# A two-layer mixer trunk: masks built first, v copied out raw before one gelu over four token tiles, and the last pair's combination moved behind a tile of u

## The chip, the cores and the metric

The kernel runs on one core of one Trainium2 chip. The metric is device time in microseconds for one execution. Besides the times there is one execution that was taken with the hardware profiler; its instruction times are what the rest of this text reads.

## The reference, cut to what matters

The program is a trunk of two residual layers over 1024 tokens of width 1024, all in float32. Layer 0 mixes the tokens in two ways that share one input projection: a gated MLP over chunks of 128 tokens (`u`, `v`), and a sliding-window attention with 8 heads and three branches of window and dilation (128, 1), (512, 4) and (2048, 16), whose outputs are weighted by the softmax of their log-denominators. The change touches only this layer's mixer.

```python
h = rms_norm(x, norm_mix_g)
# token mixer A: chunked gMLP spatial gating
u, v = gelu(u), gelu(v)
vn = layer_norm(v, ln_g, ln_b).reshape(Bn, nc, A_CHUNK, A_GROUPS, A_GROUP_DIM)
ws = where(tril, w_s, 0)
mixed = einsum('gts,bnsgc->bntgc', ws, vn) + b_s.T[:, :, None]
a = u * mixed.reshape(Bn, S, A_WIDTH)
# token mixer B: one output and one log-denominator per branch
outs, lses = dilated_branch(q, k, v, window, dilation) for each branch
b = einsum('rbhs,rbhsc->bhsc', softmax(stack(lses), axis=0), stack(outs))
x = x + concat(a, b) @ w_out
```

Behind the mixer each layer has a gated MLP with a causal convolution; layer 1 has a gated linear attention in place of this mixer.

## The kernel before, in words

Tokens are tiled by 128 (eight tiles, `NT`), the width by 128 too. Every float32 matmul operand is split into a high and a low part of a faster type (`split`, L98–101: the high part is a cast on ScalarE, L100, the low part a subtraction on VectorE, L101; for weights with a gain L105 and L106), and a product is made of three matmuls (`mm_tok`, L182–190). A scheduler orders the instructions of each engine at compile time; where `keep_in_program_order` is called on an instruction, it stays where the program has it among its engine's instructions.

`even` (L509–538) is the mixer of layer 0. It loads x, transposes it into `hq`, and then `attention` (L597–797) runs four pairs of heads. At its head stand the masks (L606–628): a memset, two GpSimd selects, an iota and nine more VectorE instructions make `mband` (window of 128) and `mboth` (the second and third branch together in the order of stride 4, where a key that both hold is counted twice). For each pair `project` (L673–732) makes q, k and v of a token tile (tile `pj`), normalises and transposes them (`tq`, `tk`), and runs the near-window attention of that tile through `unit` and `scores` (L634–667): scores in `sc`, mask and row minimum on VectorE (L643), the exponential on ScalarE (L644), transposes (`pP`, L658), and the product with v (`po`, L666). `dilated` (L734–749) does the same over the dilated order and stores its result to DRAM (`od`), from where it is read back in token order (`on`, L781). `combine` (L751–772) puts the near and the dilated part together for a group of four token tiles: the smaller of the two parts' row minima (`cM`, L756, kept in program order), differences (`cE`, L759), one exponential (L760), weights (`cD`, L763–766), two multiplications, one on GpSimd and one on VectorE (L769), an addition (L771) and a store to `bcat` in DRAM (L772). A pair's combination runs inside the next pair's projection; the last pair's is called behind the loop.

Then `gmlp` (L550–586) projects v tile by tile: gelu from PSUM on ScalarE (L567), layer normalisation (L569–576, with a power on GpSimd, L140/L141), and for each half of four tiles eight gating matmuls (`pm`, L581) whose bias adds write the result back into `mx` (L582). `u_proj` (L588–595) projects u (`pu`), takes its gelu (L592, `ut`) and multiplies it into `mx` (L593). The scheduler lets these projections overlap with the last pair's attention.

The output projection `out_first` (L434–458) reads `cat` back from `bcat` (L1110), transposes `mx` and `cat` (`pc`, L442), splits them into `hq` and multiplies with `wo` (`po`, L190 through L425). SyncE's queue (SP) issues all of these loads and stores in one order. Pools in PSUM: `pt` two buffers, `sc` two, `pj` two, `po` one, `tq` one; `pm` shares `sc` with the scores, `pc` follows in a later pool.

Of the kernel before, what the change touches and what calls it, by code (L numbers as in the profile page):

```python
# [19 lines left out]
P = 128  # L20
# [22 lines left out]
def f32(ap):  # L43
    return ap.bitcast(F32)
# [11 lines left out]
def trunk(ctx: ExitStack, tc: tile.TileContext, a, out):  # L56
# [452 lines left out]
    def even(gm_open):  # L509
        with ExitStack() as st:  # L510
            pools = {}
            for tag, bufs in (("pt", 2), ("sc", 2), ("pj", 2), ("po", 1), ("tq", 1)):
                pools[tag] = st.enter_context(tc.tile_pool(name="ps_" + tag, bufs=bufs, space=PSUM, reuse_waits="tile"))
            ps = Tagged(pools)
            pq = st.enter_context(tc.tile_pool(name="pq", bufs=1, reuse_waits="tile"))
            par0 = ExitStack()
            pq0 = par0.enter_context(tc.tile_pool(name="pq0", bufs=1, side="right", reuse_waits="tile"))
            with tc.tile_pool(name="nrm", bufs=1, reuse_waits="tile") as pool:
                for n in range(NT):
                    xt = pool.tile([P, D], F32, tag="x", bufs=3, name=f"x0{n}")  # L520
                    Q.dma_start(xt, rows(a["x"], n))
                    if n == 0:
                        Q.dma_start(g0, a["norm_mix_gT"])
                    for g in range(2):
                        pt = ps.tile([P, 4, P], F32, tag="pt", name=f"pt{n}{g}")
                        for j in range(4):
                            k = 2 * j + g
                            T.transpose(pt[:, j, :], xt[:, k * P : (k + 1) * P], ident)
                        split(place(hq[g][n // 4], n), pt)
                    if n == 1:  # L530
                        wq0 = load_qkv(0)
                    h = pool.tile([P, D], F32, tag="h", bufs=2, name=f"h{n}")
                    ssq = small.tile([P, 1], F32, tag="ssq", name=f"ssq{n}")
                    A.activation(h, xt, AF.Square, accum_out=ssq)
                    inv_rms(ssq, 1, D, f"rn{n}", r0[:, n : n + 1])
            with tc.tile_pool(name="at", bufs=2, reuse_waits="tile") as at, \
                    tc.tile_pool(name="av", bufs=1, reuse_waits="tile") as av:
                return attention(ps, at, av, pq, pq0, par0, wq0, gm_open)

    def load_qkv(p):  # L540
        return [w for kp in range(4)
# [8 lines left out]
    def gmlp(ps, gm):  # L550

        wv = load_half(a["w_vu"][0], "wv", g0)
        lnG = gm.tile([P, 512], F32, name="lnG")
        Q.dma_start(lnG, a["ln_g"].partition_broadcast(P))
        lnB = gm.tile([P, 512], F32, name="lnB")
        Q.dma_start(lnB, a["ln_b"].partition_broadcast(P))
        bs = gm.tile([P, GROUPS], F32, name="bs")
        Q.dma_start(bs, a["a_bs"])
        ws = gm.tile([P, GROUPS, P], F32, name="ws")
        Q.dma_start(ws, a["a_ws"])  # L560

        G.affine_select(out=ws, in_=ws, compare_op=ALU.is_ge, fill=0.0, base=0,
                        pattern=[[0, GROUPS], [1, P]], channel_multiplier=-1)

        def consume(n, pj):
            gv = gm.tile([P, 512], F32, tag="gv", bufs=2, name=f"gv{n}")
            A.activation(gv, pj, AF.Gelu, scale=r0[:, n : n + 1])  # L567
            st = small.tile([P, 6], F32, tag="bn", name=f"bn{n}")
            V.bn_stats(st, gv)  # L569
            mv = small.tile([P, 2], F32, tag="mv", name=f"mv{n}")  # L570
            V.bn_aggr(mv, st)
            r = inv_rms(mv[:, 1:2], 1, 1, f"lr{n}")
            V.tensor_scalar(gv, gv, mv[:, 0:1], r, op0=ALU.subtract, op1=ALU.mult)
            V.tensor_mul(gv, gv, lnG)
            half, j = n // 4, n % 4
            V.tensor_add(mx[half][:, j, :], gv, lnB)
            if j == 3:
                for g in range(GROUPS):
                    gc = mx[half][:, :, g * 64 : g * 64 + 64]
                    pm = ps.tile([P, 4, 64], F32, tag="sc", name=f"pm{half}{g}")  # L580
                    T.matmul(pm, ws[:, g, :], gc, start=True, stop=True)  # L581
                    V.tensor_scalar(gc, pm, bs[:, g : g + 1], None, op0=ALU.add)  # L582

        mx = [gm.tile([P, 4, 512], F32, name=f"mx{h}") for h in range(2)]
        proj512(ps, wv, "pv", consume)
        return [mx[n // 4][:, n % 4, :] for n in range(NT)]

    def u_proj(ps, gm, mixed):  # L588

        def consume(n, pj):  # L590
            t = gm.tile([P, 512], F32, tag="gv", bufs=2, name=f"ut{n}")
            A.activation(t, pj, AF.Gelu, scale=r0[:, n : n + 1])  # L592
            V.tensor_mul(mixed[n], mixed[n], t)  # L593

        proj512(ps, load_half(a["w_vu"][1], "wu", g0), "pu", consume)

    def attention(ps, at, av, pq, pq0, par0, wq0, gm_open):  # L597

        gqk = pq.tile([P, 2, 2, 64], F32, name="gqk", bufs=1)
        for s in range(2):  # L600
# [1 line left out]
            Q.dma_start(gqk[:, 1, s, :], a["k_g"].partition_broadcast(P))  # L602
        V.tensor_scalar(gqk[:, 0], gqk[:, 0], -0.125, None, op0=ALU.mult)
        gqk = gqk.rearrange("p a s c -> p (a s c)")

        mband = at.tile([P, 2 * P], F32, name="mband", bufs=1)  # L606
        V.memset(mband, 0.0)
        G.affine_select(out=mband[:, :P], in_=mband[:, :P], compare_op=ALU.is_ge, fill=BIG, base=0,
                        pattern=[[1, P]], channel_multiplier=-1)
        G.affine_select(out=mband[:, P:], in_=mband[:, P:], compare_op=ALU.is_ge, fill=BIG, base=0,  # L610
                        pattern=[[-1, P]], channel_multiplier=1)

        di = at.tile([P, 2 * P], I32, tag="sm", name="di", bufs=3)
        G.iota(di, pattern=[[-1, 2 * P]], base=P, channel_multiplier=1)
        V.tensor_scalar(di, di, 3, None, op0=ALU.bitwise_and)
        m16 = at.tile([P, 2 * P], F32, tag="sm", name="m16", bufs=3)
        V.tensor_copy(m16, di)
        V.tensor_scalar(m16, m16, BIG, None, op0=ALU.mult)  # L620
        V.tensor_tensor(m16[:, P:], m16[:, P:], mband[:, P:], op=ALU.max)
        mboth = at.tile([P, 2 * P], F32, name="mboth", bufs=1)
        V.tensor_tensor(mboth, mband, m16, op=ALU.min)
        count = at.tile([P, 2 * P], F32, tag="sm", name="count", bufs=3)
        V.tensor_scalar(count, mband, 1.0, None, op0=ALU.is_lt)
        V.tensor_scalar(m16, m16, 1.0, None, op0=ALU.is_lt)
        V.tensor_mul(count, count, m16)
        V.scalar_tensor_tensor(mboth, count, -math.log(2.0), mboth, op0=ALU.mult, op1=ALU.add)

        def by4(t):  # L630

# [119 lines left out]
        def combine(p, g, os):  # L751

            nm = [o[:, :, 128:130] for o in os]
            den = [o[:, :, 130:132] for o in os]
            M = small.tile([P, 4, 2], F32, tag="cM", bufs=2, name=f"cM{p}{g}")
            tc.keep_in_program_order(V.tensor_tensor(M, nm[0], nm[1], op=ALU.min))  # L756
            e = small.tile([P, 2, 4, 2], F32, tag="cE", bufs=2, name=f"cE{p}{g}")
            for i in range(2):
                V.tensor_sub(e[:, i], M, nm[i])  # L759
            A.activation(e, e, AF.Exp)  # L760
            dd = small.tile([P, 2, 4, 2], F32, tag="cD", bufs=2, name=f"cD{p}{g}")
            for i in range(2):
                V.tensor_mul(dd[:, i], e[:, i], den[i])  # L763
            V.tensor_add(dd[:, 0], dd[:, 0], dd[:, 1])
            V.reciprocal(dd[:, 1], dd[:, 0])
            V.tensor_tensor(e, e, dd[:, 1:2].to_broadcast([P, 2, 4, 2]), op=ALU.mult)
            for i, eng in ((0, G), (1, V)):
                ov = os[i][:, :, :P].rearrange("p n (s c) -> p n s c", s=2)
                eng.tensor_tensor(ov, ov, e[:, i, :, :, None].to_broadcast([P, 4, 2, 64]), op=ALU.mult)  # L769
            o0, o1 = (o[:, :, :P] for o in os)  # L770
            V.tensor_add(o0, o0, o1)  # L771
            Q.dma_start(bcat[g].rearrange("(n p) c -> p n c", p=P)[:, :, p * P : p * P + P], o0)  # L772

        made = project(0, wq0)
        for p in range(PAIRS):
# [3 lines left out]
            for g in range(2):  # L779
                on = at.tile([P, 4, 132], F32, tag="on", name=f"on{p}{g}", bufs=2)  # L780
                Q.dma_start(on, od.rearrange("(n p) c -> p n c", p=P)[:, 4 * g : 4 * g + 4, :])  # L781
                ons.append(on)

            def then(g):
                combine(p, g, [os[g], ons[g]])

            if p + 1 < PAIRS:
                made = project(p + 1, then=then)
            else:
                then(0)  # L790
                then(1)
            if p + 2 == PAIRS:
                par0.close()
                gm = gm_open()
        mixed = gmlp(ps, gm)
        u_proj(ps, gm, mixed)
        return mixed


# [448 lines left out]
```

## Time and profile before

| | before |
|---|---|
| median of 3 runs | 2196.88 us (2196.64 to 2197.8) |
| profiled execution | 2204.97 us |
| its span | 2203.2 us |
| mean granted TensorE clock | 0.992 |

The profile counts from the first to the last instruction of the program (the span). Rows of groups read: line, engine, operation, output and inputs with their shapes, count, then busy microseconds, mean nanoseconds, and the idle time ahead of them with what ended it. A row of the timeline begins with its start and its duration in microseconds. PEld is TensorE's loading of weights, which overlaps its matmuls. The granted clock is the share of the full rate that TensorE was given.

### The profile page before, as it was taken

The page shows a single profiled execution, that of the slowest core. Times are in us where ns is not written, and L with a number is a line of the kernel's source. Part 1 is how long each engine was busy: PE and PEld are TensorE (multiplying, and loading weights), DVE is VectorE, ACT ScalarE, POOL GpSimd, SP SyncE. Part 2 cuts the span into 40 slices and gives each one's busy share as a digit, 9 for nine tenths or more (in the row PEclk, how much of TensorE's full clock was granted, in tenths as well). Part 3 has the DMA queues.
Part 4 walks back from the last instruction along what each step waited for, and adds up shares of the span by engine and source line. Part 5 has one row for each costly group of instructions (what it writes and reads, how often), then busy time and mean ns, then how long its engine had stood idle before and what let it go on. Part 6 is the DMA issues. An engine that isn't in the chain of part 4 may idle for free.

```text
span 2203.2 us, 29873 instructions
## 1 busy us (share of the span) xinstructions
PE 2152.2 (98%) x10508; PEld 1820.2 (83%) x10508; DVE 1532.8 (70%) x2459; ACT 1045.5 (47%) x2006; POOL 488.0 (22%) x519
## 2 busy tenths in 40 slices
PE   7999998999999999999999999999999999999999
PEld 7999987887888888878889787878788888888887
DVE  5566654457888888845577777657787878885554
ACT  6546564345444444434453555534544444454443
POOL 4444420002333342200010011110232424320000
PEclk9999998999999999999999999999999999999999
DMA  4122212565545444575563133377544444457555
GB/s 140 51 73 80 72 42 79 174 237 181 163 158 164 159 148 161 187 281 180 202 232 113 67 99 102 105 250 267 195 139 158 154 165 158 169 176 269 204 197 195
DMA packets 157254, 349.59 MB, mean 159 GB/s; under 512 B 17408, under 2 KB 54272, under 8 KB 156720
## 3 DMA queue, kind: packets, MB, share of 16 engines
q1 hardware_dynamic: 157104, 347.68, 47.1%
q8 instruction: 83, 1.36, 0.3%
q14 instruction: 67, 0.55, 0.1%
HBM read 239.02 MB, written 108.59 MB: 158 GB/s over the span
## 4 chain that ended last, share of the span: by engine, by line
PE 83%; DMA 5%; DVE 5%; ACT 3%; issue 3%; POOL 1%; SPq 0%; ACTq 0%; DVEq 0%; POOLq 0%
PE puB L290 11%; PE pgB L290 11%; PE pgC L290 5%; PE puC L290 5%; PE pv L190 5%; PE pj L190 5%; PE pdC L397 5%; PE pdB L397 5%; PE pdO L397 4%; PE po L190 4%; PE puA L290 3%; PE pgA L290 2%; PE pdP L397 2%; PE pdQ L397 2%; PE pBq L960 2%
## 5 line engine op out<-in xcount | busy, mean ns | idle before, releaser
L101 DVE TENSOR_TENSOR da<-ar,da 128x512 fp32r<-128x512 f32 x154 | 106.3, 691 | 159.7 <-ACT da L100 159.7
L100 ACT CAST da<-ar 128x512 fp32r<-128x512 f32 x154 | 96.1, 624 | 214.3 <-PE pdC L397 98.3
L190 PE MATMUL po<-wo,hq 128*128 128x512 f32 x768 | 183.7, 394 | 1.6 <-ACT hq L100 0.9
L190 PEld LDWEIGHTS po<-wo,hq 128*128 128x128 f32 x768 | 141.7, 188 | 30.7 <-DVE hq L101 1.5
L190 PE MATMUL pj<-wq,hq 128*128 128x384 f32 x768 | 156.3, 349 | 2.2 <-ACT vN L698 1.2
L190 PE MATMUL pv<-wv,hq 128*128 128x512 f32 (+2 forms) x768 | 141.1, 340 | 2.4 <-DVE b L992 1.6
L397 PE MATMUL pdB<-dw,da 128*128 128x512 f32 x528 | 136.4, 391 | 2.1 <-ACT dw L100 2.1
L190 PEld LDWEIGHTS pj<-wq,hq 128*128 128x128 f32 x768 | 134.1, 193 | 3.9 <-ACT vN L698 2.0
L397 PE MATMUL pdC<-dw,da 128*128 128x512 f32 x528 | 136.8, 392 | 0.0
L190 PEld LDWEIGHTS pv<-wv,hq 128*128 128x128 f32 x768 | 118.7, 189 | 17.6 <-DVE b L992 2.1
L397 PEld LDWEIGHTS pdB<-dw,da 128*128 128x128 f32 x528 | 98.7, 188 | 23.4 <-ACT dw L100 2.5
L397 PEld LDWEIGHTS pdC<-dw,da 128*128 128x128 f32 x528 | 99.7, 189 | 20.7
L140 POOL TENSOR_SCALAR rn<-ssq 128x1 f32<-128x1 f32 x24 | 9.3, 386 | 478.9 <-ACT h L148 248.2
L256 POOL TENSOR_TENSOR S1g<-rg 128x512 f32<-128x512 f32 x20 | 29.2, 1462 | 384.0 <-DMA wsd<-D 251.3
L101 DVE TENSOR_TENSOR dw<-wr,dw 128x512 fp32r<-128x512 f32 x154 | 105.9, 688 | 8.6 <-ACT dw L100 8.1
L397 PE MATMUL pdO<-dw,da 128*128 128x512 f32 x396 | 102.4, 390 | 0.0
L100 ACT CAST dw<-wr 128x512 fp32r<-128x512 f32 x154 | 95.1, 617 | 11.5 <-DMA wr<-in_w_dn 7.5
L397 PEld LDWEIGHTS pdO<-dw,da 128*128 128x128 f32 x396 | 74.5, 188 | 15.6
L319 DVE SCALAR_TENSOR_TENSOR t<-g,cw,t 128x1022 f32<-128x1022 f32 x44 | 74.6, 1695 | 0.1
L318 DVE SCALAR_TENSOR_TENSOR t<-g,cw,t 128x1023 f32<-128x1023 f32 x44 | 58.3, 1325 | 16.4 <-ACT t L317 16.4
L303 DVE TENSOR_TENSOR g<-g,s1g 128x512 f32<-128x512 f32 x22 | 16.2, 738 | 73.8 <-ACT s1g L302 73.8
L320 ACT ACTIVATE t<-t 128x1024 f32<-128x1024 f32 x44 | 46.7, 1062 | 28.0 <-DVE t L319 27.9
(1070 smaller groups left out, 5422.1 us busy)
## 6 DMA issues: line engine op xcount, KB each, us to landing
ar<-actd SPq DMA_DIRECT2D x70, 512.0 KB, 3.6
rd<-in_w_down SPq DMA_DIRECT2D x44, 512.0 KB, 3.7
wsd<-D SPq DMA_DIRECT2D x88, 256.0 KB, 2.5
rg<-in_w_gate SPq DMA_DIRECT2D x42, 512.0 KB, 3.6
ru<-in_w_up SPq DMA_DIRECT2D x42, 512.0 KB, 4.6
wr<-wsd SPq DMA_DIRECT2D x40, 512.0 KB, 4.3
actd<-t SPq DMA_DIRECT2D x66, 256.0 KB, 2.2
wr<-in_w_dn SPq DMA_DIRECT2D x30, 512.0 KB, 4.9
```

The source lines that it names most:

```text
L100: (hi or A.copy)(dst[0], src)
L101: (lo or V.tensor_sub)(dst[1], src, f32(dst[0]))
L140: G.tensor_scalar(r, ssq, 1.0 / n, EPS, op0=ALU.mult, op1=ALU.add)
L190: T.matmul(o, L[i], R[jj][:, sl], start=(k == 0 and (ii, jj) == PASSES[0]), stop=(k == nk - 1 and (ii, jj) == PASSES[-1]))
L256: G.tensor_tensor(sums[name], x, y, op=op)
L290: T.matmul(o, L[ii][:, j * P : j * P + P], right[p][:, jj, j, :], skip_group_check=more, start=(not more and j == 0 and (ii, jj) == PASSES ...
L303: V.tensor_add(C22, C22, s1)
L318: V.scalar_tensor_tensor(t[:, 1:], g[:, : S - 1], w(1), t[:, 1:], op0=ALU.mult, op1=ALU.add)
L319: V.scalar_tensor_tensor(t[:, 2:], g[:, : S - 2], w(0), t[:, 2:], op0=ALU.mult, op1=ALU.add)
L320: A.activation(t, t, AF.Silu)
L397: T.matmul(o, L[ii][:, t * P : t * P + P], R[jj], skip_group_check=more, start=start and not more and (ii, jj) == PASSES[0], stop=stop and ...
L960: T.matmul(o, L[ii][:, j * P : j * P + P], right[p][:, jj, j, :], skip_group_check=more, start=(not more and j == 0 and (ii, jj) == PASSES ...
```

## The change

The masks are built by a new function `band_masks`, called at the head of `even` ahead of x, into a pool that lives as long as the attention; its temporaries sit in one tile of the weight pool. The v tiles are copied out of PSUM with their row scale but without gelu, straight into `mx`; behind the fourth tile of a half one gelu runs over all four tiles at once, and the normalisation then runs in place. The second half's gelu is kept in program order. The last pair's combination is called behind the multiplication of u's fifth tile; `combine` is cut in two, and for this pair the exponentials of both groups come first and then the rest of both. `ut` has its own five buffers instead of two shared ones.

```diff
@@ even
             pq = st.enter_context(tc.tile_pool(name="pq", bufs=1, reuse_waits="tile"))
+            masks = band_masks(pq)
...
+    def band_masks(pool):
+        mband = pool.tile([P, 2 * P], F32, name="mband", bufs=1)
+        V.memset(mband, 0.0)
+        G.affine_select(out=mband[:, :P], ...)
+        G.affine_select(out=mband[:, P:], ...)
+        t = wp.tile([P, 2, 512], F32R, tag="w", name="mtmp")
+        di, m16, count = t[:, 0, :256].bitcast(I32), f32(t[:, 0, 256:]), f32(t[:, 1, :256])
+        G.iota(di, pattern=[[-1, 2 * P]], base=P, channel_multiplier=1)
...
+        return mband, mboth
@@ gmlp
         def consume(n, pj):
-            gv = gm.tile([P, 512], F32, tag="gv", bufs=2, name=f"gv{n}")
-            A.activation(gv, pj, AF.Gelu, scale=r0[:, n : n + 1])
-            st = small.tile([P, 6], F32, tag="bn", name=f"bn{n}")
-            V.bn_stats(st, gv)
...
-            V.tensor_add(mx[half][:, j, :], gv, lnB)
-            if j == 3:
-                for g in range(GROUPS):
...
+            A.activation(mx[half][:, j, :], pj, AF.Copy, scale=r0[:, n : n + 1])
+            if j < 3:
+                return
+            ge = A.activation(flat(mx[half]), flat(mx[half]), AF.Gelu)
+            if half:
+                tc.keep_in_program_order(ge)
+            for j in range(4):
+                gv = mx[half][:, j, :]
+                st = small.tile([P, 6], F32, tag="bn", name=f"bn{half}{j}")
+                V.bn_stats(st, gv)
...
+                V.tensor_add(gv, gv, lnB)
+            for g in range(GROUPS):
...
@@ u_proj
-            t = gm.tile([P, 512], F32, tag="gv", bufs=2, name=f"ut{n}")
+            t = gm.tile([P, 512], F32, tag="ut", bufs=5, name=f"ut{n}")
             A.activation(t, pj, AF.Gelu, scale=r0[:, n : n + 1])
             V.tensor_mul(mixed[n], mixed[n], t)
+            if n == 4:
+                last()
@@ combine
             A.activation(e, e, AF.Exp)
+            return lambda: combined(p, g, os, den, e)
+
+        def combined(p, g, os, den, e):
             dd = small.tile([P, 2, 4, 2], F32, tag="cD", bufs=2, name=f"cD{p}{g}")
@@ attention
+            def weights(g):
+                return combine(p, g, [os[g], ons[g]])
             def then(g):
-                combine(p, g, [os[g], ons[g]])
+                weights(g)()
             if p + 1 < PAIRS:
                 made = project(p + 1, then=then)
-            else:
-                then(0)
-                then(1)
...
         mixed = gmlp(ps, gm)
-        u_proj(ps, gm, mixed)
+        def last():
+            for rest in [weights(g) for g in range(2)]:
+                rest()
+        u_proj(ps, gm, mixed, last)
```

More of the change, by code (lines that the diff above doesn't have):

```diff
@@ L537, in even @@
                     tc.tile_pool(name="av", bufs=1, reuse_waits="tile") as av:
-                return attention(ps, at, av, pq, pq0, par0, wq0, gm_open)
+                return attention(ps, at, av, pq, pq0, par0, wq0, masks, gm_open)
+    def band_masks(pool):
+        mband = pool.tile([P, 2 * P], F32, name="mband", bufs=1)
+        V.memset(mband, 0.0)
+        G.affine_select(out=mband[:, :P], in_=mband[:, :P], compare_op=ALU.is_ge, fill=BIG, base=0,
+                        pattern=[[1, P]], channel_multiplier=-1)
+        G.affine_select(out=mband[:, P:], in_=mband[:, P:], compare_op=ALU.is_ge, fill=BIG, base=0,
+                        pattern=[[-1, P]], channel_multiplier=1)
+        t = wp.tile([P, 2, 512], F32R, tag="w", name="mtmp")
+        di, m16, count = t[:, 0, :256].bitcast(I32), f32(t[:, 0, 256:]), f32(t[:, 1, :256])
+        G.iota(di, pattern=[[-1, 2 * P]], base=P, channel_multiplier=1)
+        V.tensor_scalar(di, di, 3, None, op0=ALU.bitwise_and)
+        V.tensor_copy(m16, di)
+        V.tensor_scalar(m16, m16, BIG, None, op0=ALU.mult)
+        V.tensor_tensor(m16[:, P:], m16[:, P:], mband[:, P:], op=ALU.max)
+        mboth = pool.tile([P, 2 * P], F32, name="mboth", bufs=1)
+        V.tensor_tensor(mboth, mband, m16, op=ALU.min)
+        V.tensor_scalar(count, mband, 1.0, None, op0=ALU.is_lt)
+        V.tensor_scalar(m16, m16, 1.0, None, op0=ALU.is_lt)
+        V.tensor_mul(count, count, m16)
+        V.scalar_tensor_tensor(mboth, count, -math.log(2.0), mboth, op0=ALU.mult, op1=ALU.add)
+        return mband, mboth
     def load_qkv(p):
@@ L565, in consume @@
         def consume(n, pj):
-            gv = gm.tile([P, 512], F32, tag="gv", bufs=2, name=f"gv{n}")
-            A.activation(gv, pj, AF.Gelu, scale=r0[:, n : n + 1])
-            st = small.tile([P, 6], F32, tag="bn", name=f"bn{n}")
-            V.bn_stats(st, gv)
[L570 to L574, printed above, removed]
-            half, j = n // 4, n % 4
-            V.tensor_add(mx[half][:, j, :], gv, lnB)
-            if j == 3:
-                for g in range(GROUPS):
[L579 to L582, printed above, removed]
+            half, j = n // 4, n % 4
+            A.activation(mx[half][:, j, :], pj, AF.Copy, scale=r0[:, n : n + 1])
[8 more added lines that the diff above has]
+                V.bn_stats(st, gv)
+                mv = small.tile([P, 2], F32, tag="mv", name=f"mv{half}{j}")
+                V.bn_aggr(mv, st)
+                r = inv_rms(mv[:, 1:2], 1, 1, f"lr{half}{j}")
+                V.tensor_scalar(gv, gv, mv[:, 0:1], r, op0=ALU.subtract, op1=ALU.mult)
+                V.tensor_mul(gv, gv, lnG)
+                V.tensor_add(gv, gv, lnB)
+            for g in range(GROUPS):
+                gc = mx[half][:, :, g * 64 : g * 64 + 64]
+                pm = ps.tile([P, 4, 64], F32, tag="sc", name=f"pm{half}{g}")
+                T.matmul(pm, ws[:, g, :], gc, start=True, stop=True)
+                V.tensor_scalar(gc, pm, bs[:, g : g + 1], None, op0=ALU.add)
         mx = [gm.tile([P, 4, 512], F32, name=f"mx{h}") for h in range(2)]
@@ L586, in gmlp, with u_proj, attention @@
         return [mx[n // 4][:, n % 4, :] for n in range(NT)]
-    def u_proj(ps, gm, mixed):
+    def u_proj(ps, gm, mixed, last):
         def consume(n, pj):
-            t = gm.tile([P, 512], F32, tag="gv", bufs=2, name=f"ut{n}")
+            t = gm.tile([P, 512], F32, tag="ut", bufs=5, name=f"ut{n}")
             A.activation(t, pj, AF.Gelu, scale=r0[:, n : n + 1])
             V.tensor_mul(mixed[n], mixed[n], t)
+            if n == 4:
+                last()
         proj512(ps, load_half(a["w_vu"][1], "wu", g0), "pu", consume)
-    def attention(ps, at, av, pq, pq0, par0, wq0, gm_open):
+    def attention(ps, at, av, pq, pq0, par0, wq0, masks, gm_open):
         gqk = pq.tile([P, 2, 2, 64], F32, name="gqk", bufs=1)
@@ L604, in attention @@
         gqk = gqk.rearrange("p a s c -> p (a s c)")
[L606 to L628, printed above, removed]
+        mband, mboth = masks
         def by4(t):
```

## The prediction

> **What bounds the kernel now.** I read the page first, then windows of 5 us over the stretch that the change touches, then the waits and the timeline inside the windows that lose time.
>
> ```profile
> span 2203.2 us, 29873 instructions
> PE 2152.2 (98%) x10508; PEld 1820.2 (83%) x10508; DVE 1532.8 (70%) x2459; ACT 1045.5 (47%) x2006; POOL 488.0 (22%) x519
> ```
>
> TensorE is busy for 98% of the span, so nothing is won by easing another engine unless TensorE waits for it, or runs at a lower granted clock behind such a wait. The profiled execution took 2204.97 us, 1.8 us more than its span and 8.1 us (0.37%) more than the median of the runs, 2196.88. The sum below is a difference against the profiled one and is then laid on the median.
>
> The windows' columns are PE, PEld, DVE, ACT and POOL busy time, then the granted clock, the DMA share and GB/s.
>
> ```profile
> 40.00:45.00 5.00, 2.85 (x22) 2.15 (x20) 4.93 (x14) 2.75 (x7) 3.40 (x7) 0.97 0.01 3
> 45.00:50.00 5.00, 2.73 (x12) 2.35 (x11) 4.96 (x17) 1.69 (x7) 1.67 (x3) 0.50 0.01 3
> 50.00:55.00 5.00, 5.00 (x29) 5.00 (x28) 2.70 (x8) 3.59 (x12) 0.65 (x1) 0.50 0.00 0
> 145.00:150.00 5.00, 4.33 (x23) 3.83 (x24) 2.10 (x7) 2.53 (x8) 3.42 (x6) 0.71 0.28 86
> 150.00:155.00 5.00, 5.00 (x19) 5.00 (x19) 1.29 (x4) 1.28 (x5) 1.98 (x4) 0.60 0.17 52
> 340.00:345.00 5.00, 3.08 (x9) 2.56 (x10) 3.72 (x11) 4.95 (x12) 0.74 (x2) 0.67 0.91 249
> 370.00:375.00 5.00, 2.35 (x6) 1.31 (x5) 4.04 (x15) 0.43 (x2) 1.55 (x1) 0.74 0.10 30
> 375.00:380.00 5.00, 3.87 (x10) 2.52 (x9) 4.05 (x12) 2.55 (x3) 0.93 (x1) 0.50 0.08 22
> 380.00:385.00 5.00, 5.00 (x18) 4.06 (x17) 0.69 (x1) 0.00 (x0) 0.57 (x1) 0.73 0.52 145
> ```
>
> Three stretches lose time in two ways: TensorE is idle, and after the idle it works at about half clock. At 40–55 VectorE is full for ten microseconds and TensorE loses 2.15+2.27 = 4.4 idle. Counting busy time times the missing clock, 2.73×0.5+5×0.5 plus a rest is another 3.9. At 340–345 ScalarE is full; the loss is 1.92 idle plus 3.08×0.33 = 2.9. At 370–385, idle is 2.65+1.13 = 3.8 and the clock takes 2.35×0.26+3.87×0.5+5×0.27 = 3.9, together 7.7. The change acts on all three, and makes a fourth.
>
> **Part 1, masks first.** Ten VectorE instructions build the masks at 40–48; these are the dearest and the cheapest of the ten, which sum to 4.4 us.
>
> ```profile
> L621 DVE TENSOR_TENSOR m<-m,mband 128x128 f32<-128x128 f32 x1 | 0.8, 764 | 0.0
> ...
> L607 DVE MEMSET mband<- 128x256 f32 x1 | 0.3, 272 | 0.0
> ...
> 6.16 0.69 DVE L101 TENSOR_TENSOR hq<-pt,hq 128x512 fp32r<-128x512 f32 x1 [4.54 <-ACT hq L100]
> ...
> 56.89 2.62 PE L190 MATMUL pj<-wq,hq 128*128 128x384 f32 x14
> ```
>
> In the compiled order of the changed kernel they stand ahead of VectorE's first subtraction for `hq`, where VectorE idles for 4.54 us (third row). So 4.4 us fit, at worst 0.5 us late because GpSimd's iota and two selects interleave, while TensorE waits for x; on GpSimd these three come before its first norm, which also waits for x. Without that cover it would be 4.4 us on the path. TensorE's idle at 40–50 is of the same size, 4.4. Walking the new order by these durations, the projection tile that starts at 56.89 starts near 49.5, but 2.2 us of score and transpose work that was ahead of it now stands behind: 7.4−2.2, about 5, if the clock stays up. If it falls as now, about 2. A floor of 0 holds if the projection's own normalisation chain fills VectorE anyway; the ceiling is 6.5, most of the 8.3 lost. I take **−3** (0 to −6.5), nearer to the falling clock, since some idle stays and the fall came early in the idle.
>
> **Part 2, v raw and one gelu for four tiles.** Compiled, the stretch from the v tiles to the end of u has 10 activation-table loads where it has 21 now:
>
> ```profile
> L644 ACT ACT_TABLE_LOAD x9 | 11.5, 1283 | 12.1 <-DVE ot3d L643 6.5 <-DVE ot3n L643 5.5
> L567 ACT ACT_TABLE_LOAD x8 | 10.3, 1283 | 0.1
> L592 ACT ACT_TABLE_LOAD x3 | 3.8, 1283 | 0.9 <-DVE mx L593 0.8
> L760 ACT ACT_TABLE_LOAD x1 | 1.3, 1283 | 0.0
> 404.14 0.69 ACT L592 ACTIVATE ut<-pu,r 128x512 f32<-128x512 f32 x1
> L320 ACT ACTIVATE t<-t 128x1024 f32<-128x1024 f32 x44 | 46.7, 1062 | 28.0 <-DVE t L319 27.9
> ...
> PE pP3d L658 <- ACT sm3d L644: 3.3, 3, 2.1
> 280.00:335.00 55.00, 53.19 (x286) 44.22 (x285) 29.34 (x75) 35.01 (x62) 9.23 (x20) 1.00 0.08 22
> ```
>
> Eleven loads are 11×1.283 = 14.1 us of ScalarE, an engine that TensorE waits for through the dilated exponentials only 3.3 us in all (row of `pP3d`), 2.1 of it in the one wait at 340. In 280–335 TensorE idles 1.8 us in all (last row). So v before 335 gives **−1.5** (0 to −1.8). What appears in return is a block on ScalarE: load, gelu over 128x2048 (an estimate of 1.8 us: 0.69 for a gelu of 512 columns, 1.062 for an activation of 1024, 0.37 for each 512 more), load: 4.4 us in which no exponential of attention can start. TensorE has u matmuls to issue in it, so I cost it at nothing here; without them it is the last rival.
>
> Although the text of the change speaks of the second gelu behind the last exponential, the compiled order has it ahead of the last eight.
>
> The Trainium skill, ScalarE: Activation LUTs, What ACT_TABLE_LOAD costs, gives the load 1283 ns and a drain of about 1380 ns more at each switch. Here an exponential starts as its load ends (the timeline row at 340.08, below), so no drain stands behind it; by the page the eleven would free 29 us of ScalarE rather than 14.
>
> **Part 3, the two stretches in u.**
>
> ```profile
> 340.08 1.28 ACT L644 ACT_TABLE_LOAD   x1
> 341.37 0.40 ACT L644 ACTIVATE sm3d<-sm3d,ot3d 128x128 f32<-128x128 f32 x1
> 341.92 0.48 PE L658 MATMUL pP3d<-ident,sm3d 128*128 128x128 f32 x1 [2.07 <-ACT sm3d L644]
> ...
> 369.56 0.17 DVE L756 TENSOR_TENSOR cM<-ot3n,on 128x8 f32<-128x8 f32 x1 [2.91 <-DMA on<-od]
> 371.26 1.55 POOL L769 TENSOR_TENSOR ot3n<-ot3n,cE 128x512 f32<-128x512 f32 x1 [29.41 <-DVE cE L766]
> 372.35 1.19 PE L581 MATMUL pm<-mx,ws 128*128 128x256 f32 x2 [2.14 <-DVE mx L582]
> 374.06 2.07 PE L581 MATMUL pm<-mx,ws 128*128 128x256 f32 x4 [0.51 <-DVE mx L582]
> 377.26 6.90 PEld L190 LDWEIGHTS pu<-wu,hq 128*128 128x128 f32 x20 [1.85 <-ACT ut L592]
> 384.20 0.86 PEld L581 LDWEIGHTS pm<-mx,ws 128*128 128x128 f32 x4
> 385.09 4.53 PEld L190 LDWEIGHTS pu<-wu,hq 128*128 128x128 f32 x20
> ```
>
> The wait at 340 is on an exponential behind a table load behind a gelu. At 370 the last pair's combination, kept in program order, sits on VectorE ahead of the bias adds that free the gating matmuls' PSUM (cM at 369.56, pm waits 2.14 and 0.51), and u's gelus wait in turn. Counted by instructions instead of windows: 369.8 to 384.2 holds six gating matmuls (1.3 us at 0.86/4 each) and twenty of u (4.53 undisturbed, last row), so 14.4−5.8 = 8.5 are lost; with 3.7 at 340 (2.1 idle, then half clock until about 345) that is 12.2, against 10.6 by the windows. The combination leaves this place and `ut` has five buffers, so VectorE and ScalarE no longer bunch here. I take **−11.5**, allowing up to 0.7 for fresh waits behind the gelu block; bounds −8 (a third of it returns) and −12.8.
>
> **Part 4, the seam to the output projection.** Compiled, `cM` of the last pair follows the multiplication of u's tile 4, which needs the last gating matmul; TensorE issues that one only behind u's tile 7. So the combination overlaps no u matmul. It starts when TensorE has only two transposes of `mx` left and needs `cat`, which is read from `bcat`.
>
> ```profile
> 395.96 0.48 DVE L582 TENSOR_SCALAR mx<-pm,bs 128x256 f32<-128x256 f32 x1 [4.53 <-PE pm L581]
> 403.72 0.37 PEld L442 LDWEIGHTS pc<-ident,mx 128*128 128x128 f32 x2
> 405.24 1.08 ACT L100 CAST hq<-pc 128x512 fp32r<-128x512 f32 x2
> 408.36 3.01 PE L190 MATMUL po<-wo,hq 128*128 128x512 f32 x12
> ...
> cat<-bcat SPq DMA_DIRECT2D x6, 256.0 KB, 3.1
> od<-ot3d SPq DMA_DIRECT2D x4, 132.0 KB, 4.4
> bcat<-ot3n SPq DMA_DIRECT2D x2, 256.0 KB, 2.4
> ```
>
> From the end of the last gating matmul: its bias add 0.5; on VectorE four multiplications and one weight subtraction, queued with the combination's first half, five times the 0.69 of the row at 6.16, 3.4; small ones and the exponential as at 369.56 to 371.26, some 2.3 with the second group's share; GpSimd's 1.55; the addition 0.69. That is 8.4. Then the store 2.4 and the load 3.1: 13.9. SP now issues the loads of `wo10` to `wo13` ahead of these stores, and all that follows on SP (`cat`, `xh`, `qg`) waits behind them. From `cat` on, transposes, cast and subtraction take about what 405.24 to 408.36 took, 3.1, and 0.4 for transposes: 17.4. Now the same way takes 403.72 to 408.36 = 4.6. Added wait: 12.8. Such an idle lowers the clock: at 40–55, 4.4 us of idle were followed by 10 us near half; at 340–345 some 3. I take 5 us at half, 2.5 lost, so **+15.3**. Lower bound +11 (parts of the VectorE chain done while TensorE still works, no lost clock), upper +17.5 (both landings a microsecond longer).
>
> The Trainium skill, TensorE: Matmul & The Clock Gate, The HAM clock gate, speaks against this seam: half rate after an idle window of about 3.4 us, back after a busy one of 3.4. The rows differ: 1.92 us of idle were enough at 340, and 7 or more busy ones at half followed at 45–55. By the page the seam's clock costs 3.4×0.5 = 1.7, and the sum falls by 0.8.
>
> **Sum:** −3 −1.5 −11.5 +15.3 = −0.7 on the profiled execution (2204.3), and **2196.2** on the median.
>
> **The rivals.**
>
> Slower, the seam is longer: both landings like the slow row (`od`, 4.4 instead of 2.4; `cat` 2.1 longer, as it goes out just behind four `wo` loads) add 4.1, and ten microseconds at half clock as at 45–55 add 2.5: 2196.2+6.6 = 2202.8. For: those loads precede on the queue. Against: in the present seam `cat` lands unhurried. It decides once the seam costs over 20.4 (15.3+0.7+4.4).
>
> Faster, the clock stays up: VectorE eased at 40–55 leaves idles too short to set it off, 3.5 more, and the dip at 145–155, where the clock alone loses 4.33×0.29+5×0.4 = 3.3, does not recur with a shifted schedule: about 2189. For: the falls follow idles. Against: the dip at 145 comes behind only 0.67 us.
>
> Faster, ScalarE sets the pace in v and u: all of 14.1 counts instead of the 5.2 that parts 2 and 3 give to ScalarE (1.5+3.7): 2187. Against: only 3.3 us of waits on these exponentials.
>
> The batching doesn't do what it says: the last eight exponentials wait behind load, gelu and load, TensorE has run out of u tiles' PSUM, and 2.5 to 4.5 of part 3 come back: about 2199.5.
>
> **How the numbers follow.** A change within 0.2% (4.4 us) is what measurement can't tell from none. Chances: the forecast 0.40 (its own range 2190.9 to 2201.5, the terms' half-widths 3.2, 0.9, 2.4 and 3.2 added in squares), slower 0.29, clock up 0.18, ScalarE 0.08, batching 0.05. Each is split at 2192.5 and 2201.3 by its own spread, in the order named. Faster: 0.05+0.16+0.08 = 0.29. Same: 0.31+0.05+0.02+0.04 = 0.42. Slower: 0.04+0.24+0.01 = 0.29. All low ends sum to 2186.8, all high ends to 2206.4; the range 2187 to 2206 is cut where little is left out.
>
> **What would show it.** After: the masks before 7 us with TensorE's start unmoved; VectorE under full at 40–50; ten table loads; no wait of `pP3d` over 1 us; no clock under 0.9 between 335 and 385; then TensorE idle for 10 us or more ahead of the transposes of `cat`, released by DMA. If that gap is under 6 us, or a new stall above 3 us stands behind the big gelu, the forecast is wrong, and so it is if the start slips with the masks.

## The result and the profile after

The changed kernel took 2199.13 us (median of 20 runs, 2195.31 to 2204.81) against 2195.90 for the kernel before (20 runs, 2189.64 to 2200.19). The ratio is 1.0016, with a 95% interval of 1.0009 to 1.0024: 3.5 us slower, not the 0.7 us faster that the sum gave. That is inside the stated range and within 0.2%, but a ratio of 1, no change at all, lies outside the interval, and the sign is the other one. The profiled executions say 2201.7 us of span after and 2203.2 before, the other way round, so one execution against one can't tell 3 us here.

What did the three old stretches become? These are the windows of 5 us of the changed kernel, columns as in the prediction.

```profile
40.00:45.00 5.00, 4.33 (x34) 3.76 (x32) 4.02 (x14) 3.20 (x9) 2.67 (x6) 1.00 0.00 2
45.00:50.00 5.00, 4.47 (x38) 3.94 (x37) 4.44 (x14) 3.43 (x12) 2.61 (x5) 1.00 0.02 5
...
145.00:150.00 5.00, 4.84 (x20) 4.84 (x21) 2.03 (x7) 2.33 (x8) 3.27 (x5) 0.50 0.05 13
...
340.00:345.00 5.00, 5.00 (x29) 4.22 (x27) 5.00 (x13) 3.42 (x9) 0.36 (x1) 1.00 0.18 54
...
375.00:380.00 5.00, 5.00 (x24) 4.15 (x23) 0.97 (x2) 0.00 (x0) 0.00 (x0) 1.00 0.00 0
...
390.00:395.00 5.00, 0.00 (x0) 0.00 (x0) 4.90 (x20) 0.43 (x2) 2.22 (x2) 0.57 0.45 147
395.00:400.00 5.00, 0.00 (x0) 0.00 (x0) 1.97 (x2) 0.00 (x0) 0.82 (x1) 0.50 0.37 107
400.00:405.00 5.00, 2.04 (x6) 1.40 (x7) 0.94 (x2) 1.07 (x2) 0.00 (x0) 0.50 0.73 232
405.00:410.00 5.00, 5.00 (x21) 4.16 (x20) 1.73 (x3) 1.17 (x2) 0.00 (x0) 0.72 0.77 273
476.00:481.00 5.00, 0.91 (x5) 0.52 (x4) 1.88 (x3) 1.15 (x2) 1.22 (x3) 0.85 0.72 258
481.00:486.00 5.00, 5.00 (x18) 4.43 (x17) 3.45 (x7) 3.25 (x8) 0.74 (x2) 0.50 0.14 52
```

At 340 and 375 TensorE is full at full clock. The seam is there, ten microseconds with no matmul at all. And there is a stretch that the prediction never named, 476 to 486: TensorE busy for 0.91 of 5 us and then at half clock. The same place in the kernel before, in its windows:

```profile
474.00:479.00 5.00, 3.31 (x22) 2.64 (x21) 2.70 (x4) 1.34 (x3) 0.88 (x3) 1.00 0.19 64
479.00:484.00 5.00, 5.00 (x28) 4.18 (x27) 3.61 (x6) 3.22 (x9) 0.74 (x2) 1.00 0.15 56
```

The view of waits of the changed kernel (engine, line, what it waited for, us in total, times, longest) names both places; the third row is SyncE's queue (SPq):

```profile
PE pc L442 <- DMA cat<-bcat: 14.0, 1, 14.0
PE pt L162 <- DVE xt L152: 4.1, 1, 4.1
...
SPq L497 <- DMA xd<-xh: 6.5, 1, 6.5
```

Before, the wait on `xt` was 1.7 us, and that load waited 0.3 us for `xd`:

```profile
PE pt L162 <- DVE xt L152: 1.7, 1, 1.7
...
SPq L497 <- DMA xd<-xh: 0.3, 1, 0.3
```

To see where time was won and lost I took the start of TensorE's first matmul of each tile (24 matmuls to a tile, counted off in the trace). The table has the time in the kernel before, and the shift against it in the other profiled executions; the runs in the other columns are described below.

| first matmul of | before, at | after | no_gelu | gelu_only | comb_old | after_qr | before_pad |
|---|---|---|---|---|---|---|---|
| projection, pair 1, tile 0 | 72.2 | −2.2 | −4.3 | +0.2 | −3.9 | −4.5 | +0.5 |
| projection, pair 3, tile 6 | 265.3 | −1.5 | −3.8 | −2.7 | −3.0 | −4.3 | −2.9 |
| u, tile 3 | 362.8 | −10.2 | −4.0 | −11.4 | −11.6 | −12.9 | −4.2 |
| u, tile 5 | 386.2 | −19.0 | −14.2 | −13.4 | −20.5 | −21.7 | −4.6 |
| output, first half, tile 2 | 419.2 | +0.3 | +4.3 | −13.4 | −15.7 | −3.0 | −4.6 |
| output, second half, first tile | 456.4 | −0.3 | +3.7 | −13.4 | −16.5 | −3.8 | −4.4 |
| output, second half, fifth tile | 481.4 | +6.4 | +8.0 | −14.2 | −11.9 | −3.2 | −1.4 |
| end of the span | 2203.2 | −1.5 | +1.9 | −18.3 | −19.9 | −8.0 | −8.7 |

By the fifth tile of the second half the changed kernel is 6.4 us behind. From there to the end every column gains 4 to 8 us, also those with nothing changed in that part but the time at which it starts: it is the profiled execution of the kernel before that was slow there, so the last row is not read as an effect of the change. One column alone is not good to a few us either: `before_pad` runs the order of the kernel before and is 2.9 us ahead of it at pair 3, and a second execution of the changed kernel (after_again, below) has −6.9 there in place of −1.5. Differences between two rows of one column repeat better.

### The profile page after: what moved, and what is told of

It reads as the page before. It is cut to its first block, busy times and chain, and to the rows that moved or that the text cites. A ratio compares the mean times of both kernels' runs of the same rounds, so it can differ in the third digit from the quotient of the medians.

```text
span 2201.7 us, 29848 instructions
## 1 busy us (share of the span) xinstructions
PE 2148.4 (98%) x10508; PEld 1817.6 (83%) x10508; DVE 1536.1 (70%) x2459; ACT 1032.4 (47%) x1997; POOL 490.9 (22%) x519
## 4 chain that ended last, share of the span: by engine, by line
PE 71%; DMA 4%; DVE 2%; ACT 1%; issue 1%; POOL 0%; SPq 0%; ACTq 0%; DVEq 0%
PE puB L290 11%; PE pgB L290 11%; PE pgC L290 5%; PE puC L290 5%; PE pdB L397 5%; PE pdC L397 5%; PE pv L190 4%; PE pdO L397 4%; PE po L190 4%; PE puA L290 3%; PE pgA L290 2%; PE pdQ L397 2%; PE pdP L397 2%; PE pBq L977 2%; PE pBr L977 2%; DMA xd<-xt 1%
## 5 line engine op out<-in xcount | busy, mean ns | idle before, releaser
L397 PEld LDWEIGHTS pdC<-dw,da 128*128 128x128 f32 x528 | 99.0, 188 | 20.5
L100 ACT CAST dw<-wr 128x512 fp32r<-128x512 f32 x154 | 95.0, 617 | 15.7 <-DMA wr<-in_w_dn 10.8
```

The lines of the kernel that those rows point to most:

```text
L100: (hi or A.copy)(dst[0], src)
L397: T.matmul(o, L[ii][:, t * P : t * P + P], R[jj], skip_group_check=more, start=start and not more and (ii, jj) == PASSES[0], stop=stop and ...
```

## The experiments

The theory after the result is that the prediction's three terms stand and that a term is missing: a load of `xt` that waits for an unrelated store because the larger pool moved the buffers (*the layout*). Its rival is that the loss at 476 is a chance dip, and that the seam or the gains were mis-sized. The compiled program says something about the first already. This is the load in the kernel before, and in the changed one, with what it waits for:

```
before  L497 DMACopy xt00<-xd00 128x512 [waits DMAHW5, PE]
after   L497 DMACopy xt00<-xd00 128x512 [waits DMAHW5, DMAHW3, PE]
```

Three more buffers for `ut` are 6 KB per partition in the pool that holds `mx`. The output projection's pool is placed next to that one and moves by as much. The addresses in the compiled programs bear the theory out: in the kernel before, the first buffer of `xt` lies over the two buffers of `cat`, which have long been read; in the changed one it lies also over both buffers of `xh`, and DMAHW3 is the store of the last `xh` to `xd`. The load must wait until that store has read its buffer. The moved pool adds waits elsewhere too. One of them is in the seam: the first load of `cat` now waits for the stores of both groups, though it reads the first group's alone.

**after_again** is the changed kernel once more, with no edit.

> The changed kernel once more, as the yardstick of this group of runs and as a second look at what follows the seam. Theory (the layout): the first load of xt behind the output projection waits about 6 us for the store of xh to land, so TensorE again idles about 4 us near 478 and has some 7 us at half clock behind it; ratio to before 1.001 to 1.003. Rival (a chance dip of one execution): that load waits under 1 us, TensorE idles under 2 us there and no half clock follows; the ratio is then carried by the seam alone.

Ratio 1.0010 (1.0000 to 1.0019), inside the theory's range. The waits in its own profile are the same, so it is no dip of one execution:

```profile
SPq L497 <- DMA xd<-xh: 6.1, 1, 6.1
...
PE pc L442 <- DMA cat<-bcat: 13.9, 1, 13.9
PE pt L162 <- DVE xt L152: 4.4, 1, 4.4
```

**before_pad** adds the space alone to the kernel before. Every engine's compiled order is that of the kernel before; the load has the extra wait, and so has the first load of `cat`.

```diff
-        mx = [gm.tile([P, 4, 512], F32, name=f"mx{h}") for h in range(2)]
+        mx = [gm.tile([P, 4, 512], F32, name=f"mx{h}") for h in range(2)] + [gm.tile([P, 1536], F32, name="pad")][:0]
```

> The kernel before with 6 KB per partition of unused space in the pool that holds mx, as much as the change added there with three more buffers for ut; nothing else. Theory (the layout): the first xt buffer now lies where an earlier tile lay, the compiled load waits for one more DMA, and the kernel is 3 to 6 us slower: ratio 1.0014 to 1.0027, with a wait of 4 to 8 us on SP ahead of that load. Rival: the space has no effect, ratio within 0.9995 to 1.0005.

Ratio 1.0018 (1.0006 to 1.0030), 4.0 us, inside the theory's range. SyncE's queue waits there too, as its timeline shows (start, duration, instruction):

```profile
457.48 0.75 SPq L430 DMA_DIRECT2D xd<-xh  x1
458.60 0.40 SPq L110 DMA_DIRECT2D rg<-in_w_gate  x1
465.10 0.33 SPq L497 DMA_DIRECT2D xt<-xd  x1
```

The store goes out at 457.48, and 6.1 us after the load of `rg` was issued the load of `xt` may go. TensorE's wait on `xt` rises to 3.3 us; the table's column loses 3.0 us between the first and the fifth tile. Empty space, never written or read, costs 4 us.

```profile
PE pt L162 <- DVE xt L152: 3.3, 1, 3.3
```

**after_qr** takes the opposite way: one line makes the output projection's pool begin with the raw side weights, so that these and a buffer of `cat`, all read by then, lie under `xt` instead of `xh`. The compiled order of every engine is that of the changed kernel.

```diff
+            pool.tile([P, D], F32, tag="qr", bufs=2, name="qr") if l == 0 else None
             def cat0(n):
```

> The changed kernel with one line more: the output projection's pool opens with the buffers of its raw side weights instead of those of cat and xh. Every engine's compiled order is the changed kernel's; the first xt load has no DMA wait of another tile. Theory (the layout): 3 to 6 us less than the changed kernel, ratio to before 0.9975 to 1.0000, SP waits under 1 us for xd ahead of that load, TensorE under 2.5 us for xt. Rival: the ratio stays at 1.001 or above.

Ratio 0.9999 (0.9989 to 1.0009), inside the theory's range. The wait for `xd` ahead of that load falls to 0.3 us and TensorE's to 1.8. The seam stays; its wait is a microsecond shorter, as the first load of `cat` no longer waits for the second group's store:

```profile
SPq L497 <- DMA xd<-xh: 0.3, 1, 0.3
...
PE pc L442 <- DMA cat<-bcat: 13.0, 1, 13.0
PE pt L162 <- DVE xt L152: 1.8, 1, 1.8
```

**after_u3** gives `ut` three buffers, which also keeps the load free of the wait, at the price of another order of the gating matmuls.

```diff
-            t = gm.tile([P, 512], F32, tag="ut", bufs=5, name=f"ut{n}")
+            t = gm.tile([P, 512], F32, tag="ut", bufs=3, name=f"ut{n}")
```

> The changed kernel with three buffers for ut instead of five. Theory (the layout): the first xt load does not wait for the store of xh, 3 to 6 us less than the changed kernel, ratio to before 0.9980 to 0.9996; the seam's wait for cat stays at about 14 us. Rival: too few buffers, u's gelus hold TensorE by several us, ratio 1.001 or more.

Ratio 0.9998 (0.9988 to 1.0008), just above the theory's range, with 13.2 us of wait for `cat` and 1.5 for `xt`. So the layout's price is 4.0 us on the kernel before, and 2.4 to 4.0 on the changed one (1.0016 or 1.0010 against 0.9999 and 0.9998). On the changed kernel each pair's intervals overlap or just touch; all go the same way.

**masks_only** is part 1 on the kernel before.

```diff
+            masks = band_masks(pq)
             par0 = ExitStack()
...
-        mband = at.tile([P, 2 * P], F32, name="mband", bufs=1)
...
+        mband, mboth = masks
```

> The kernel before with part 1 alone, the masks built at the head. Theory (the prediction's part 1): TensorE's start does not move, the projection tile that started at 56.89 starts near 50, and 2 to 5 us are gained, ratio 0.9977 to 0.9991. Rival (the work only moves): the gain is given back behind that tile, ratio 0.9995 or more.

Ratio 0.9989 (0.9978 to 0.9999), 2.4 us less: inside the theory's range, though the interval reaches into the rival's. In its profile the clock stays at 1.00 from 40 to 55, where it had been 0.50 for ten microseconds, and the projection tile of 56.89 starts at 50.0; but by pair 1 only 2.8 us are left, so most of what that tile gained is given back, as the rival said.

**gelu_only** is part 2 on the kernel before.

```diff
-            A.activation(gv, pj, AF.Gelu, scale=r0[:, n : n + 1])
...
+            A.activation(mx[half][:, j, :], pj, AF.Copy, scale=r0[:, n : n + 1])
+            if j < 3:
+                return
+            ge = A.activation(flat(mx[half]), flat(mx[half]), AF.Gelu)
...
```

> The kernel before with part 2 alone: v raw, one gelu for four tiles, normalisation in place; the combination and the two buffers of ut stay. Theory (ScalarE off the path at 340): the wait of pP3d goes, 1.5 for v and 3.7 at 340, about 5 us less, ratio 0.9970 to 0.9985, and 370 to 385 keeps its loss. Rival (ScalarE sets the pace): most of the 14.1 us of loads, ratio 0.9935 to 0.9955. Second rival (the block of load, gelu, load delays the last exponentials): no gain, ratio 0.9990 or more.

Ratio 0.9959 (0.9944 to 0.9975), 9.0 us less, between the first theory and its rival: almost twice the 5.2 that I gave it (the interval says 5.5 to 12.3), and less than the 12.8 us of table loads that went (21 to 11, by the groups of ScalarE). The normalisation is batched by this edit too, so not all of it need be ScalarE's. In the table it gains 8.7 between pair 3 and u's tile 3, then 2.0 up to tile 5. The longest wait that remains of the loss at 370 is one behind the combination:

```profile
362.86 0.17 DVE L761 TENSOR_TENSOR cM<-ot3n,on 128x8 f32<-128x8 f32 x1 [1.25 <-DMA on<-od]
362.94 0.48 DVE L587 TENSOR_SCALAR mx<-pm,bs 128x256 f32<-128x256 f32 x1
...
363.47 0.70 PE L586 MATMUL pm<-mx,ws 128*128 128x256 f32 x2 [1.11 <-DVE mx L587]
```

These are rows of its timeline: `cM` waits for its DMA, the bias add behind it waits, and TensorE for the bias add.

**no_gelu** is the changed kernel without part 2: `consume` of `gmlp` as before.

```diff
+            A.activation(gv, pj, AF.Gelu, scale=r0[:, n : n + 1])
...
-            ge = A.activation(flat(mx[half]), flat(mx[half]), AF.Gelu)
...
```

> The changed kernel with v's gelu tile by tile as before: masks and the moved combination alone. Theory (the loss at 340 and most of 370 to 385 was the gelu's): masks 2 to 4 us less, the seam 12 to 17 more, the layout 3 to 5 more, the loss at 370 to 385 only partly gone: ratio 1.0030 to 1.0080. Rival (the prediction's part 3: the combination's leaving frees 8.5 us by itself): ratio 1.0000 to 1.0025.

Ratio 1.0043 (1.0025 to 1.0061), inside the theory's range, but not for its reason. The windows at 370 to 385 are full at full clock, and the column gains 10.2 us between tiles 3 and 5: the combination's leaving, with the five buffers of `ut`, did free the 8.5 us of the prediction, and more, without the gelu's help. Which of the two did it no run shows. The wait of 2.1 us on the exponential at 340 is there as before. What makes the run slow is the seam, 13.7 us of wait for `cat`, and the layout, 4.5 us on SyncE.

```profile
370.00:375.00 5.00, 5.00 (x24) 4.14 (x23) 1.74 (x4) 0.69 (x1) 0.00 (x0) 1.00 0.00 0
375.00:380.00 5.00, 5.00 (x24) 4.14 (x23) 0.97 (x2) 0.69 (x1) 0.00 (x0) 1.00 0.00 0
```

**comb_old** is the changed kernel with the combination where it was.

```diff
-            if n == 4:
-                last()
...
                 made = project(p + 1, then=then)
+            else:
+                then(0)
+                then(1)
```

> The changed kernel with the last combination where the kernel before calls it, ahead of gmlp. Theory (the sum): no seam, 15 to 17 us less, but the loss at 370 to 385 comes back with some 8.5; 6 to 9 us under the changed kernel, ratio to before 0.9970 to 0.9990. Rival (the loss at 370 needed the old gelus too): it doesn't come back, 13 to 17 us less, ratio 0.9930 to 0.9955.

Ratio 0.9949 (0.9933 to 0.9965), 14.7 us under the changed kernel by the two ratios (13.4 by that of after_again); the theory of the plain sum falls and its rival's range holds. The loss at 370 doesn't come back: between u's tiles 3 and 5 this column gains 8.9, with the combination in the old place. Its timeline shows the same pieces on VectorE, while TensorE waits for none of them:

```profile
366.56 0.69 DVE L781 TENSOR_TENSOR ot3n<-ot3n,on 128x512 f32<-128x512 f32 x1 [0.94 <-POOL ot3n L779]
367.18 0.16 DVE L762 TENSOR_TENSOR cM<-ot3n,on 128x8 f32<-128x8 f32 x1
367.25 0.48 DVE L611 TENSOR_SCALAR mx<-pm,bs 128x256 f32<-128x256 f32 x1
...
367.80 2.49 DVE L622 TENSOR_TENSOR mx<-mx,ut 128x512 f32<-128x512 f32 x4
```

Four multiplications run in a row: four tiles of `ut` had been waiting in buffers of their own while TensorE went on. `gelu_only` has two buffers and 2.0 us of idle at 360 to 365. The two runs differ in the buffers and the masks, so the five buffers are the likely cause; that is not shown, for a run with the buffers alone was not made.

**last3** calls the combination behind u's fourth tile, which hangs on first-half gating matmuls only.

```diff
-            if n == 4:
+            if n == 3:
                 last()
```

> The changed kernel with the last combination behind u's fourth tile instead of the fifth, so that it hangs on no second-half gating matmul. Theory (the seam): the wait of TensorE for cat, 14.0 us, goes, and with it the half clock behind it: 13 to 17 us under the changed kernel, ratio to before 0.993 to 0.996. Rival (VectorE in order): the combination holds up the bias adds again, as near 370 in the kernel before, and 6 to 9 us come back: ratio 0.997 to 0.999.

Ratio 0.9950 (0.9938 to 0.9962); 2184.11 us against 2196.00 of the changed kernel in the same group, 11.9 less, somewhat under the 13 to 17; the ratio is inside the theory's range. No wait for `cat` shows, and the rival's stall at 370 doesn't either: one tile earlier, and the seam is gone.

**last3_u3** has three buffers for `ut` beside it.

> The run before this one with three buffers for ut instead of five, which keeps the compiled load of xt free of the extra DMA wait. Theory (the layout): another 3 to 6 us less than with five, ratio to before 0.990 to 0.994. Rival (too few buffers): u's gelus wait for their buffers, TensorE waits for PSUM, and it is 1 to 4 us slower than with five.

Ratio 0.9940 (0.9927 to 0.9952), 3.2 us less in the medians, the intervals overlapping. The theory's wait goes: none on `xt` is left in its list. Against the rival the run is not slower; but counted as in the table from pair 3's tile 6 on, its one trace has lost 2.0 us against five buffers by the second half's first tile (clock 0.93 from 385 to 410), and why was not followed up.

**last3_qr** and **comb_old_qr** add the one line of after_qr.

> The combination behind u's fourth tile, with the same one line. Theory (seam and layout together): 13 to 18 us for the seam and 3 to 6 for the layout, ratio to before 0.9905 to 0.9935, the fastest so far. Rival: the layout's wait was covered there, ratio 0.9940 to 0.9955 as without the line.

> The combination at its old place, masks and gelu as changed, with the same one line. Theory (moving the combination gains nothing that the gelu batch and five buffers for ut don't): ratio 0.9915 to 0.9940, level with the run behind u's fourth tile within 3 us. Rival (the place matters): over 4 us slower than that run.

Ratios 0.9941 (0.9926 to 0.9956) and 0.9938 (0.9922 to 0.9953), medians 2180.72 and 2178.43. The last is the fastest here, 14.9 us under the kernel before in its group, but not clear of the other runs without a seam. The line is worth 2.0 and 2.4 us by ratios whose intervals overlap, less than the 3 to 6 expected, so last3_qr fell into its rival's range; TensorE's wait on `xt` was 0.4 us in it against 4.4 in last3. That the two places for the combination are level within 3 us held, and the ratio of comb_old_qr is inside its theory's range.

## Why the prediction was wrong

Measured on the profiled execution, part by part. For the two middle terms the mark is where TensorE begins to transpose `mx` for the output projection. These rows are from the timelines of the kernel before,

```profile
403.94 0.38 PE L442 MATMUL pc<-ident,mx 128*128 128x128 f32 x2
```

and of the changed one, with the end of the seam:

```profile
387.49 0.48 DVE L611 TENSOR_SCALAR mx<-pm,bs 128x256 f32<-128x256 f32 x1
388.00 0.69 DVE L622 TENSOR_TENSOR mx<-mx,ut 128x512 f32<-128x512 f32 x1
388.02 0.66 PE L442 MATMUL pc<-ident,mx 128*128 128x128 f32 x4 [0.67 <-DVE mx L611]
...
388.61 0.16 DVE L764 TENSOR_TENSOR cM<-ot3n,on 128x8 f32<-128x8 f32 x1
...
394.84 2.13 DVE L783 TENSOR_TENSOR ot3n<-ot3n,on 128x512 f32<-128x512 f32 x2
...
396.40 0.98 SPq L784 DMA_DIRECT2D bcat<-ot3n  x2
399.98 0.33 SPq L1127 DMA_DIRECT2D cat<-bcat  x1
...
402.71 0.90 PE L442 MATMUL pc<-ident,cat 128*128 128x128 f32 x3 [14.03 <-DMA cat<-bcat]
```

| term | predicted | measured |
|---|---|---|
| masks (up to pair 3) | −3 | −1.5 here, −2.4 alone by the runs |
| v and u (up to 388.02: −15.9, less the masks) | −13.0 | −14.4 |
| seam (from −15.9 to −0.3 at the second half's start) | +15.3 | +15.6 |
| sum | −0.7 | −0.3; −0.2 by the runs of after_qr (−2.4 to +2.0) |
| layout | not in the sum | +6.7 here, 2.4 to 4.0 by the runs |

The changed kernel's second execution, after_again, gives −6.9 for the masks, −14.5 for v and u, +14.7 for the seam and +6.5 for the layout. So all but the masks repeat to a microsecond, and with the masks the sum does not: that the first trace comes so near to −0.7 is luck, and it is the runs of after_qr that bear the sum out. Why the runs make the layout cheaper than the traces do is open.

*The step that failed* is in part 3: five buffers for `ut` were booked as help alone, and their layout stood in the sum at nothing. They are what makes the pool 6 KB larger, and the price, 2.4 to 4.0 us by the runs, falls some 90 us later, on a load in another pool. With the extra waits of the layout taken away and no instruction moved, the changed kernel is level with the kernel before, as the sum had it; with them, it is slower. The prediction looked for what the change adds in the compiled order of the instructions, and this addition changes no order. It shows in the waits of the compiled program, as the listing above has it.

*Part 1* held in its mechanism: the masks fit into the idle start, the tile of 56.89 came 6.4 us earlier, the clock stayed up from 40 to 55. Most of that went again at 60 to 73, behind a wait of 1.9 us of `po` on VectorE's copy of `pT` and a short stretch of lower clock (0.83 over 70 to 80; in after_again it is 1.00 there). This give-back the prediction did not have; its −3 lies near the 2.4 of masks_only, whose interval (0.2 to 4.8) can't tell the two prices of the prediction, 2 and 5, apart.

*Parts 2 and 3* were right together and wrong in their shares. The 8.5 us at 370 were had in two ways, both with five buffers: by moving the combination without the one gelu (no_gelu, 10.2 between tiles 3 and 5), and by keeping it in place with the one gelu (comb_old, 8.9). The prediction gave them to the move. So in the changed kernel the move bought nothing that was not there already, and its seam is a loss in full: 14.7 us between comb_old and the changed kernel.

*Part 4* held nearly step by step. The chain from the last bias add to the end of the first addition took from 387.49 to 395.53 (394.84 and 0.69), 8.0 where 8.4 was summed. The first store was issued at 396.40, about 1 us later than the addition ended, and the load of `cat` at 399.98. That is 3.6 us where 2.4 was summed, not because a store was slow (they landed in 2.4 and 2.6 us) but because the load waited for the second group's store as well, the layout's other wait; SyncE's queue waited 2.2 us for it. In after_qr, without that wait, the load went 2.7 us behind the first store and TensorE's wait was 13.0, so about 1 us of the seam belongs to the layout. `cat` took 2.7 against 3.1.

```profile
SPq L1127 <- DMA bcat<-ot3n: 2.2, 1, 2.2
```

TensorE's wait came to 14.0. The time lost to the lower clock behind it is 2.04×0.5+5×0.28 = 2.4, against 2.5 in the prediction.

*The rivals.* The slower one named a longer seam, the wrong place: the store and load together were a microsecond off, not four. "The clock stays up" came true at 40 to 55. The dip at 145 recurred in this execution (0.50 there) but not in after_again (1.00); before_pad, which has the order of the kernel before, has none either, so that this dip comes and goes between executions and is no work of the change. It is part of why one trace is not good to a few us. ScalarE may have set more of the pace than 5.2: 9.0 by gelu_only. The last one, exponentials behind the block, did not happen: no wait of `pP3d` is left in the list of the changed kernel's waits.

## What to carry to other kernels

A larger buffer count can also shift what is placed behind it: compare the waits of the compiled program, not only its order, and where a transfer has a new wait on an unrelated store, ask which buffer lies there; reordering two allocations took it away here. Where the other parts of a change already cure a stall, one more cure is worth nothing, so price each part with the others in place. A step with a DRAM round trip behind it belongs ahead of the last work that can cover it: one tile earlier was worth 12 us here. And one trace against another is good for a few us only between two marks of the same execution.

## What the runs showed of the hardware

A 256 KB store of `xd` lands in 2.4 us at the median in the kernel before. The last such store of the first half, with loads of 512 KB issued on both sides of it, let the waiting load go only 8.1 us after its issue; in the kernel before the same store took 7.6 us, and nothing waited for it. The rows are SyncE's timeline in the changed kernel:

```profile
461.53 0.52 SPq L430 DMA_DIRECT2D xd<-xh  x1
462.73 0.33 SPq L110 DMA_DIRECT2D rg<-in_w_gate  x1
469.63 0.33 SPq L497 DMA_DIRECT2D xt<-xd  x1
```

In the seam TensorE had its clock lowered while it idled: from 390 to 395 it was granted 0.57 with no matmul at all, so that for a wait of 14 us only 2.4 us were lost to the clock, about as much as behind the wait of 4.1 us at 476 to 486 (5.00×0.50 = 2.5). A wait of that kind is not always followed by a fall: `before_pad` waits 3.3 us in the same place and keeps 1.00 from 465 to 500, and its wait of 2.1 us on `pP3d`, behind which the kernel before had 0.67, leaves the clock at 1.00 as well.
